# Second attention block: input projections with 512 moving weight columns, and the work between attention units dealt out anew

## The chip, the cores and the metric

One core of a Trainium2 chip runs the whole program in one launch. The metric is the device time of one execution in microseconds (us). Kernels are compared by the median of several runs.

## What is computed

The program is a chain of two transformer blocks on 512 tokens of width D = 1024, in fp32. The first block (attention with a convolution branch, then an expert layer) isn't touched here and takes the first 1866 us. The second block is this, cut to what matters:

```
h = rms_norm(x, norm_g)                       # 512 x 1024
proj = h @ w_in                               # mq mk mv mg (512 each), dq dk dv dg (512 each)
mq, mk = rms_norm per head of 64              # 8 heads
m_out = moba_attention(mq, mk, mv, slopes) * silu(mg)
dq, dk = rms_norm per component of 64         # 4 heads x 2 components
d_out = diff_attention(dq, dk, dv, lam)       # (softmax(q1 k1) - lam softmax(q2 k2)) v, causal, ALiBi
d_out = rms_norm(d_out, diff_subln) * 0.8 * silu(dg)
x = x + concat(m_out, d_out) @ w_out
```

## The kernel before, in words

Every product in fp32 is made of three TensorE matmuls on parts in the type fp32r: high x high, high x low and low x high. A weight block is loaded by DMA (`wraw`), ACT makes its high part (`whi`, L76) and DVE its low part (`wlo`, L77), both in `split`. The normed input of the second block lies transposed, feature chunk by feature chunk, in `h3h` and `h3l` (eight chunks k of 128 features by 512 tokens); they are made at the start of the block from `h3t` (L914), ACT for the high part, DVE for the low part.

The block's projections are generators, whose `yield`s are the steps in which they are dealt out. `head64` makes q or k of two head pairs (256 weight columns) for all four token tiles: `nat` (L82 to L98) takes 128 tokens as the stationary operand and 256 weight columns as the moving one, with two token tiles in each of two PSUM banks. Then come squares (ACT) with a sum (DVE), `rsq` (a square root on ACT, which loads another table, and small DVE steps), and `qn` (L973, DVE); `turn64` transposes `qn` on PE (L987) and writes qT or kT in two parts. `vals` makes v in the same way, without a norm. `gates` makes a block of 128 gate features for all 512 tokens (L113 to L115, the weights stationary and 512 token columns moving) and ends with Silu on ACT.

The attention is cut into 32 units: the kind (m, d), the head pair or diff head j (0 to 3), and the query tile qt (0 to 3). `score` makes two score tiles (three matmuls each on PE, L1027, then bias and maximum on DVE, L1032, Exp on ACT, L1036, and scaling on DVE). `turn` transposes the probabilities (L1068), and ACT copies them to `cpt`. After qt = 3, `finish` multiplies with v (`pv`, L1077 or L1081). For a diff head it has a chain of its own: `do` (ACT), `dsq` (ACT square), `ones_sum` (PE, L143), `diag` (DVE, four `ddj`, L151), `rsq` (ACT root, L125, and DVE), `bcast_rows` (PE, L137, of `drr`), then two products on DVE and the split into `mxd`. The mixed heads are multiplied with w_out: six of eight chunks in `part_out`, the last two in the last stage.

The loop over the units works two units of scores ahead (L = 2) and between them takes steps of the generators in `fill`: a number of steps `work[i]`, dealt evenly over the units up to `ends[i]`. Only q, k, v of the first pairs and gate 0 are made ahead of the loop. What stands on an engine's queue follows this order, with priorities by which a scheduler moves instructions past each other. PSUM has eight banks: three for `pm` (projections, ones, bcast, outputs), two for `s` (scores), two for `t` (turns), one for `o`.

Of the kernel before, what the change touches and what calls it, by code (L numbers as in the profile page):

```python
# [11 lines left out]
F32 = mybir.dt.float32  # L12
F32R = mybir.dt.float32r
# [17 lines left out]
def block_mixer_kernel(ctx: ExitStack, tc: tile.TileContext, a, out, dbg=None, stop=None):  # L31
# [8 lines left out]
    def pm(tag="pm"):  # L40
        return ps[0].tile([128, 512], F32, name=tag, tag=tag, bufs=ps[1][tag] if isinstance(ps[1], dict) else ps[1])
# [46 lines left out]
    def nat(src, jobs):  # L88


        for i in range(2):
            hi, lo = wsplit(src[:, 4 * i:4 * i + 4, :], 4, 256)
            for n, (o, x) in enumerate(jobs):
                for k in range(4):
                    (xh, xl), f, l = x(4 * i + k), i + k + n % 2 == 0, 4 * i + k == KD - 1
                    P.matmul(o, xh, hi[:, k, :], start=f, stop=False, skip_group_check=True)  # L96
                    P.matmul(o, xh, lo[:, k, :], start=False, stop=False, skip_group_check=True)  # L97
                    P.matmul(o, xl, hi[:, k, :], start=False, stop=l, skip_group_check=True)  # L98
                if n % 2:
# [175 lines left out]
    def tok(src, t):  # L275
        return lambda k: src(k, slice(t * 128, t * 128 + 128))
# [672 lines left out]
    p4x_tag = ["pm", "s"]

    def p4x():
        tag = p4x_tag[0]
        p4x_tag.append(p4x_tag.pop(0))
        p = [pm(tag), pm(tag)]
        return p, [(p[t // 2][:, t % 2 * 256:t % 2 * 256 + 256], tok(hx3, t)) for t in range(NT)]

    def head64(nm, b, base, gcol):

        pp, jobs = p4x()
        yield from nat(a["w_in_2n"][base + b], jobs)  # L960
        q2 = pc.tile([128, 2, 2, T], F32R, name=nm + "T", tag="T_%s%d" % (nm[1], b))
        qk[nm, b] = q2
        ss = sm.tile([128, 16], F32, name="ss64", tag="hss", bufs=2)
        for t2 in range(2):
            sq = sb.tile([128, 512], F32, name="sq64", tag="tmp", bufs=4)
            S.activation(sq, pp[t2], AF.Square)
            V.tensor_reduce(ss[:, 8 * t2:8 * t2 + 8], sq.rearrange("p (h d) -> p h d", d=64), axis=AX.X, op=OP.add)
        V.tensor_scalar(ss, ss, 1.0 / 64, EPS, op0=OP.mult, op1=OP.add)
        r = rsq(ss, 16, "r64")
        qn = []  # L970
        for t2 in range(2):
            q = sb.tile([128, 512], F32, name="qn64", tag="tmp", bufs=4)
            V.tensor_tensor(q.rearrange("p (h d) -> p h d", d=64), pp[t2].rearrange("p (h d) -> p h d", d=64),  # L973
                            r[:, 8 * t2:8 * t2 + 8, None].to_broadcast([128, 8, 64]), op=OP.mult)
            qn.append(q)
        late.append((nm, q2, qn, gcol))

    late = []

    def turn64():  # L980
        while late:
            nm, q2, qn, gcol = late.pop(0)
            for t2 in range(2):
                p2 = pm("t")
                for i in range(2):
                    for c in range(2):
                        P.transpose(p2[:, (c * 2 + i) * 128:(c * 2 + i) * 128 + 128],  # L987
                                    qn[t2][:, i * 256 + c * 128:i * 256 + c * 128 + 128], ident)
                hi = q2[:, :, 0, t2 * 256:t2 * 256 + 256]
                lo = q2[:, :, 1, t2 * 256:t2 * 256 + 256]  # L990
                p3 = p2.rearrange("p (c q) -> p c q", c=2)
                S.activation(hi, p3, AF.Copy, scale=g64[:, gcol:gcol + 1])
                V.scalar_tensor_tensor(lo, p3, g64[:, gcol:gcol + 1], hi.bitcast(F32), op0=OP.mult, op1=OP.subtract)

    def vals(nm, b, base):
        pp, jobs = p4x()
        yield from nat(a["w_in_2n"][base + b], jobs)
        v = pc.tile([128, NT, 256], F32, name=nm + "s", tag="T_v%d" % b)
        vs[nm, b] = v
        for t2 in range(2):  # L1000
            S.activation(v[:, 2 * t2:2 * t2 + 2, :], pp[t2].rearrange("p (t n) -> p t n", t=2), AF.Copy)

    def gates(j):
        w = wfeat(a["w_in_2f"][j])
# [11 lines left out]
    def both(kind, j, qt, btab):  # L1016


        w_ = (qt + 1) * 128
        wm_ = max(w_, 256)  # L1020
        q_, k_ = (qk[kind + z, j // 2][:, j % 2] for z in "qk")
        qs = slice(qt * 128, qt * 128 + 128)
        s = [pm("s"), pm("s")]
        for n, (x, y) in enumerate(((0, 0), (0, 1), (1, 0))):
            for half in range(2):
                r = slice(half * 64, half * 64 + 64)
                P.matmul(s[half][:, :wm_], q_[r, x, qs], k_[r, y, :wm_], start=n == 0, stop=n == 2)  # L1027
        r_ = []
        for half in range(2):
            st = sm.tile([128, 4], F32, name="ast", tag="ast", bufs=8)  # L1030
            e = pc.tile([128, 512], F32, name="e2", tag="e2", bufs=8)
# [77 lines left out]

    def chain(*gens):  # L1110
        for g_ in gens:
            for n, _ in enumerate(g_):
                if n == 1:
                    turn64()
                yield
        turn64()

    mxm = sb.tile([128, 2, 4, T], F32R, name="mxm", tag="xs")
    mxd = {}
    run(chain(head64("mq", 0, 0, 0), head64("mk", 0, 2, 1), vals("mv", 0, 4), gates(0)))  # L1120
# [5 lines left out]
    def part_out(j):  # L1126
# [6 lines left out]
        for k in range(6):  # L1133
# [13 lines left out]
    cur, done, total, n0, n1 = iter(()), 0, 0, 0, 1
# [78 lines left out]
def _pack(i):  # L1226
# [30 lines left out]
    p["w_in_2n"] = _blk(np.concatenate([w[:, :1536], w[:, 2048:3584]], 1), 256)  # L1257
# [22 lines left out]
```

## Time and profile before

| | |
|---|---|
| median of 3 runs | 2186.14 us (2185.35 to 2186.24) |
| the profiled execution | 2186.87 us, span 2184.9 us |
| granted clock, mean of the span | 0.991 |
| PE busy in the span | 2138.0 us (98%) |
| DVE, ACT busy in the span | 1688.1 us (77%), 1053.9 us (48%) |

The second block runs from about 1866 us to the end. Times in the rows below are microseconds from the span's start. In the timeline, "idle before" tells for how long an engine stood idle ahead of an instruction and which instruction released it. A busy PE is not PE at its peak: the ends of matmuls are modelled, so the spacing of the starts is what counts. The granted clock is a share of the full 2.4 GHz.

### The profile page before, as it was taken

Reading aid. Unit: us, or ns where it says so; the run is one execution under the profiler, and the core shown is the slowest. Engines: PE = TensorE matmul, PEld = TensorE weight load, DVE = VectorE, ACT = ScalarE, POOL = GpSimd, SP = SyncE. Lnnn points to the kernel's source line nnn. Section 1 sums busy time; section 2 is a strip of 40 time slices with the busy share of each in tenths; the row PEclk is TensorE's granted clock in tenths of the full one; section 3 lists DMA queues with packets and bytes.
Section 4 is the critical chain, followed back from the end, with each engine's and each line's share of the span. In section 5 each row is a group of like instructions: output and inputs, shape, how many; then the busy total and the mean of one; then the engine's idle time right before and its main releaser. Section 6 shows DMA issues by size and latency. Waiting matters only on the chain.

```text
span 2184.9 us, 31138 instructions
## 1 busy us (share of the span) xinstructions
PE 2138.0 (98%) x11665; PEld 1864.3 (85%) x11665; DVE 1688.1 (77%) x3340; ACT 1053.9 (48%) x1923; POOL 158.9 (7%) x132
## 2 busy tenths in 40 slices
PE   7999999999999899999999999999999999999999
PEld 3899888877688899998988889988989887888876
DVE  3999997576799999767777777787777765755564
ACT  3344367642433488734444444444443444466672
POOL 0000000000000000011111221111111100000000
PEclk9999999999999999999999999999999999999999
DMA  7322450167333266788888898898888874322221
GB/s 272 119 78 88 135 180 14 45 221 256 137 96 101 76 225 256 286 326 313 320 319 318 313 323 307 314 334 309 320 303 314 314 250 155 112 82 88 73 75 65
DMA packets 150870, 449.50 MB, mean 206 GB/s; under 512 B 12096, under 2 KB 69184, under 8 KB 131520
## 3 DMA queue, kind: packets, MB, share of 16 engines
q1 hardware_dynamic: 132288, 313.30, 41.8%
q0 software_dynamic: 18432, 134.23, 16.2%
q8 instruction: 91, 1.49, 0.3%
q14 instruction: 59, 0.48, 0.1%
HBM read 407.51 MB, written 39.98 MB: 205 GB/s over the span
## 4 chain that ended last, share of the span: by engine, by line
PE 88%; DVE 7%; ACT 2%; DMA 2%; issue 1%; SPq 0%; DVEq 0%; ACTq 0%
PE pda L770 16%; PE pm L113 9%; PE pm L115 9%; PE pm L114 9%; PE pdb L770 8%; PE pda L113 3%; PE pda L115 3%; PE pda L114 3%; PE pda L729 3%; PE pdb L113 2%; PE pdb L115 2%; PE pdb L114 2%; PE pm L430 2%; PE pm L96 2%; PE pm L97 2%; PE pm L98 2%
## 5 line engine op out<-in xcount | busy, mean ns | idle before, releaser
L76 ACT ACTIVATE whi<-wraw 128x1024 fp32r<-128x1024 f32 (+1 forms) x254 | 266.3, 1049 | 349.1 <-PE pda L114 117.5
L113 PE MATMUL pm<-h2h,whi 128*128 128x384 f32 x1024 | 347.2, 339 | 2.9 <-ACT gn L623 2.9
L77 DVE TENSOR_TENSOR wlo<-wraw,whi 128x1024 fp32r<-128x1024 f32 (+1 forms) x254 | 307.2, 1210 | 53.1 <-ACT whi L76 52.1
L115 PE MATMUL pm<-h2h,wlo 128*128 128x384 f32 x1024 | 345.1, 337 | 0.1
L114 PE MATMUL pm<-h2l,whi 128*128 128x384 f32 x1024 | 344.5, 336 | 0.0
L783 POOL DMA_INDIRECT uv<-in_peer_uv,eid x128 | 158.7, 1240 | 1606.9 <-ACT xt L724 910.4
L77 DVE TENSOR_TENSOR vvl<-vraw,vvh 128x1024 fp32r<-128x1024 f32 x128 | 156.6, 1223 | 110.7 <-ACT vvh L76 110.7
L113 PEld LDWEIGHTS pm<-h2h,whi 128*128 128x128 f32 x1024 | 193.8, 189 | 7.0 <-ACT gn L623 3.3
L114 PEld LDWEIGHTS pm<-h2l,whi 128*128 128x128 f32 x1024 | 193.7, 189 | 3.6
L115 PEld LDWEIGHTS pm<-h2h,wlo 128*128 128x128 f32 x1024 | 193.3, 189 | 0.3 <-DVE wlo L77 0.3
L814 DVE SCALAR_TENSOR_TENSOR xt<-uv,zz,xt 128x1024 f32<-128x1024 f32 x128 | 164.0, 1282 | 13.8 <-ACT zz L813 13.8
L76 ACT ACTIVATE ah<-gn 128x384 fp32r<-128x384 f32 x93 | 48.9, 526 | 232.7 <-DVE gn L756 197.5
L770 PE MATMUL pda<-vvh,ah 128*128 128x512 f32 x512 | 158.3, 390 | 0.0
L770 PE MATMUL pda<-vvl,ah 128*128 128x512 f32 x512 | 158.0, 390 | 0.0
L770 PE MATMUL pda<-vvh,al 128*128 128x512 f32 x512 | 157.6, 389 | 0.0
L786 DVE SCALAR_TENSOR_TENSOR xt<-uv,xn 128x1024 f32<-128x1024 f32 x128 | 155.9, 1218 | 0.0
L76 ACT ACTIVATE vvh<-vraw 128x1024 fp32r<-128x1024 f32 x128 | 134.5, 1051 | 5.1 <-PE pm L114 3.2
L770 PEld LDWEIGHTS pda<-vvh,ah 128*128 128x128 f32 x512 | 96.1, 188 | 21.1
L770 PEld LDWEIGHTS pda<-vvl,ah 128*128 128x128 f32 x512 | 96.1, 188 | 20.7
L770 PEld LDWEIGHTS pda<-vvh,al 128*128 128x128 f32 x512 | 96.1, 188 | 20.4
L623 ACT ACTIVATE gn<-pm 128x384 f32<-128x384 f32 x115 | 56.0, 487 | 116.4 <-PE pm L115 115.0
L77 DVE TENSOR_TENSOR al<-gn,ah 128x384 fp32r<-128x384 f32 x93 | 52.6, 565 | 66.5 <-ACT ah L76 66.5
(523 smaller groups left out, 4862.9 us busy)
## 6 DMA issues: line engine op xcount, KB each, us to landing
wraw<-in_peer_uT SPq DMA_DIRECT2D x128, 512.0 KB
vraw<-in_peer_uv SPq DMA_DIRECT2D x128, 512.0 KB
w_d<-wst SPq DMA_DIRECT2D x12, 2048.0 KB
wcur<-w_d SPq DMA_DIRECT2D x31, 768.0 KB
wraw<-in_w_in_f SPq DMA_DIRECT2D x32, 512.0 KB
mraw<-in_w_modT SPq DMA_DIRECT2D x24, 512.0 KB
wraw<-in_w_in_2n SPq DMA_DIRECT2D x24, 512.0 KB
fw<-in_w_mod SPq DMA_DIRECT2D x16, 512.0 KB
```

Source lines behind the costliest of these rows:

```text
L76: S.activation(hi, src, AF.Copy)
L77: V.tensor_tensor(lo, src, hi.bitcast(F32), op=OP.subtract)
L96: P.matmul(o, xh, hi[:, k, :], start=f, stop=False, skip_group_check=True)
L113: P.matmul(o, lh, rh, start=first, stop=False)
L114: P.matmul(o, lh, rl, start=False, stop=False)
L115: P.matmul(o, ll, rh, start=False, stop=last)
L623: S.activation(g_, p[:, :ND], AF.Gelu)
L729: P.matmul(p[:, q * 128:q * 128 + 128], o0[:, q], o1[:, q], start=True, stop=True)
L770: P.matmul(yp[t][:, d * 512:d * 512 + 512], x[:, t * 128:t * 128 + 128], v[:, d * 512:d * 512 + 512], start=j == 0 and n == 0, stop=j == N ...
L783: G.indirect_dma_start(out=uv, out_offset=None, in_=a["peer_uv"], in_offset=bass.IndirectOffsetOnAxis(ap=eid[:, s_:s_ + 1], axis=0))
L786: V.scalar_tensor_tensor(junk, uv[:, :D], 1.0, xn, op0=OP.mult, op1=OP.mult, accum_out=zs)
L814: V.scalar_tensor_tensor(y0, uv[:, D:], cs, y0, op0=OP.mult, op1=OP.add)
```

## The change

The input projections of the second block for q, k and v come in six blocks of 512 weight columns instead of twelve of 256. `nat512` walks over the token tiles outside: each token tile has a PSUM bank of its own, and the block's weights stay in four chunks, which are made while token tile 0 runs. `heads64` makes q and k together, with the norm for every two token tiles; `turn64` comes two steps later (`late`, `tick`). `vals` makes v of all four pairs. Ahead of the loop only q, k of the first pairs and gate 0 are made; v follows in the first stretch of the loop. The fill has three stretches instead of four (from units 0, 8 and 24), and gates 6 and 7 come in the last, ahead of the output steps. v of m and d have buffers of their own; `e2` has seven buffers instead of eight. The weights are packed in the new order on the host.

```diff
+    def nat512(n, done):
+        w = []
+        for t in range(NT):
+            o = pm()
+            for c in range(4):
+                if t == 0:
+                    w.append(wsplit(a["w_in_2n"][n][:, 2 * c:2 * c + 2, :], 2, 512))
+                for k in range(2):
+                    mm3(o, tok(hx3, t)(2 * c + k), [z[:, k, :] for z in w[c]], c + k == 0, c + k == 4)
+                if c == 1:
+                    yield
+            done(t, o)
+            yield
...
-        for t2 in range(2):
-            S.activation(v[:, 2 * t2:2 * t2 + 2, :], pp[t2].rearrange("p (t n) -> p t n", t=2), AF.Copy)
+        def done(t, o):
+            for b in range(2):
+                S.activation(vs[kind + "v", b][:, t, :], o[:, b * 256:b * 256 + 256], AF.Copy)
...
     def chain(*gens):
         for g_ in gens:
-            for n, _ in enumerate(g_):
-                if n == 1:
+            for _ in g_:
+                tick[0] += 1
+                if late and late[0][-1] <= tick[0] - 2:
                     turn64()
                 yield
-        turn64()
...
-    run(chain(head64("mq", 0, 0, 0), head64("mk", 0, 2, 1), vals("mv", 0, 4), gates(0)))
+    run(chain(heads64("m", 0, 0), gates(0)))
...
-    fill = {0: chain(head64("mq", 1, 0, 0), head64("mk", 1, 2, 1), gates(1), vals("mv", 1, 4), gates(2), gates(3)),
-            8: chain(head64("dq", 0, 6, 2), head64("dk", 0, 8, 3), vals("dv", 0, 10), gates(4), gates(5)),
-            16: chain(head64("dq", 1, 6, 2), head64("dk", 1, 8, 3), vals("dv", 1, 10), gates(6), gates(7)),
-            25: chain(*(part_out(j) for j in range(KD)))}
-    ends = {0: 8, 8: 16, 16: 25, 25: 38}
-    work = {0: 18, 8: 16, 16: 16, 25: 8}
+    fill = {0: chain(vals("m", 1), heads64("m", 1, 2), gates(1)),
+            8: chain(gates(2), heads64("d", 0, 3), gates(3), vals("d", 4), gates(4), heads64("d", 1, 5), gates(5)),
+            24: chain(gates(6), gates(7), *(part_out(j) for j in range(KD)))}
+    ends = {0: 8, 8: 24, 24: 36}
+    work = {0: 18, 8: 32, 24: 12}
...
+        while late and i + L in (8, 16, 24):
+            turn64()
         if i + L < len(units):
             e[i + L] = score(units[i + L])
```

Three pieces of the engines' order follow: the line, the operation, the tiles and the shape. The line numbers are those of the kernel that the piece comes from; after the change L96 to L98 become L113 to L115, and the others move by 14 to 16.

PE at the finish of diff head 0, before: `o` is `pv`, `ones` the sum, `drr` the broadcast; `pm<-whi,h3h` and its like are projections.

```order
L1077 MATMUL o<-cpt,dvs 128x128
L1068 MATMUL t<-ident,e_18138 128x128
L987 MATMUL t<-ident,qn_18252 128x128 x4
L96 MATMUL pm<-whi,h3h 128x256
...
L987 MATMUL t<-ident,qn_18254 128x128 x4
L143 MATMUL pm<-dsq,ones 128x512
L97 MATMUL pm<-wlo,h3h 128x256
...
L1027 MATMUL s<-dkT,dqT 128x512 x6
L1068 MATMUL t<-ident,e_18218 128x128 x2
L1068 MATMUL t<-ident,e_18297 128x128 x3
L1027 MATMUL s<-dkT,dqT 128x256 x10
L137 MATMUL pm<-ident,drr 128x128 x4
```

The same place after the change:

```order
L1093 MATMUL o<-cpt,dvs 128x128
L1084 MATMUL t<-ident,e_17546 128x128
L1043 MATMUL s<-dkT,dqT 128x512 x6
L1001 MATMUL t<-ident,qn_17681 128x128 x4
L1001 MATMUL t<-ident,qn_17683 128x128 x4
L143 MATMUL pm<-dsq,ones 128x512
L1043 MATMUL s<-dkT,dqT 128x256 x2
L1084 MATMUL t<-ident,e_17623 128x128 x2
L1043 MATMUL s<-dkT,dqT 128x256 x10
L137 MATMUL pm<-ident,drr 128x128 x4
L113 MATMUL pm<-whi,h3h 128x512
```

Before, 10 projection matmuls stood ahead of the sum and 14 between the sum and the broadcast; after, they all stand behind the broadcast.

ACT at the same finish, before: `do` and `dsq` of the chain, `drt` the root, `e` the Exp of scores (its number tells the tile), `r64t` the root for q and k.

```order
L125 ACTIVATE r64t<-ss_18237 128x16
L1036 ACT_TABLE_LOAD
L1036 ACTIVATE e_18297,ast<-e_18297,ast 128x384
L1036 ACTIVATE e_18300,ast<-e_18300,ast 128x384
L1092 ACTIVATE do<-o 128x512
L1069 ACTIVATE cpt<-t 128x128
L1094 ACTIVATE dsq<-do 128x512
L992 ACTIVATE dkT<-t,g_15885 128x2x256 x2
L1001 ACTIVATE dvs<-pm 128x512
L125 ACT_TABLE_LOAD
L125 ACTIVATE drt<-ddv 128x4
```

And after the change:

```order
L1052 ACTIVATE e_17697,ast<-e_17697,ast 128x384
L1085 ACTIVATE cpt<-t 128x128
L1052 ACTIVATE e_17792,ast<-e_17792,ast 128x512
L1108 ACTIVATE do<-o 128x512
L1052 ACTIVATE e_17795,ast<-e_17795,ast 128x512
L1110 ACTIVATE dsq<-do 128x512
L1006 ACTIVATE dqT<-t,g_15885 128x2x256
L1006 ACTIVATE dkT<-t,g_15885 128x2x256
L1085 ACTIVATE cpt<-t 128x2x128
L1052 ACTIVATE e_17877,ast<-e_17877,ast 128x128
L1052 ACTIVATE e_17880,ast<-e_17880,ast 128x128
L125 ACT_TABLE_LOAD
```

Two Exps of 512 columns now stand ahead of `dsq`, and two of 128 with a copy ahead of the root's table; the copy `dvs` and one `dkT` are gone from between.

PE at the finish of diff head 1, after the change; `pm<-h3h,whi` and its like are gate 6.

```order
L1093 MATMUL o<-cpt,dvs 128x128
L1084 MATMUL t<-ident,e_17877 128x128
L115 MATMUL pm<-h3h,wlo 128x512
L113 MATMUL pm<-h3h,whi 128x512
...
L143 MATMUL pm<-dsq,ones 128x512
L1043 MATMUL s<-dkT,dqT 128x512 x6
L1084 MATMUL t<-ident,e_17936 128x128 x2
L1084 MATMUL t<-ident,e_17982 128x128 x3
L1043 MATMUL s<-dkT,dqT 128x256 x12
L1043 MATMUL s<-dkT,dqT 128x384 x6
L1043 MATMUL s<-dkT,dqT 128x512 x3
L137 MATMUL pm<-ident,drr 128x128 x4
```

Ten matmuls of gate 6 stand between `pv` and the sum, where before there were only scores and turns; the other 14 of gate 6 stand ahead of `pv`, and gate 7 behind the broadcast.

## Rows read from the trace of the kernel before

**Rows 1.** Windows: us; busy of PE, PEld, DVE, ACT, POOL (instructions); PEclk; DMA share; GB/s.

```profile
1867.00:1877.00 10.00, 9.89 (x60) 9.60 (x61) 9.88 (x19) 5.55 (x10) 0.00 (x0) 0.71 0.01 2
1912.00:2075.00 163.00, 161.85 (x1205) 142.11 (x1204) 92.72 (x258) 107.79 (x202) 0.00 (x0) 1.00 0.26 81
2075.00:2092.00 17.00, 16.82 (x117) 13.56 (x117) 13.93 (x53) 14.37 (x27) 0.00 (x0) 1.00 0.24 82
2105.00:2130.00 25.00, 22.51 (x96) 14.96 (x95) 17.43 (x76) 19.84 (x44) 0.00 (x0) 0.86 0.11 32
2121.95:2128.78 6.83, 6.82 (x19) 4.90 (x19) 5.46 (x23) 4.42 (x13) 0.00 (x0) 0.50 0.01 2
```

**Rows 2.** Groups by line of PE, 1866 to 2185 us: shapes, count | busy, mean ns | idle.

```profile
L96 PE MATMUL pm<-whi,h3h 128*128 128x256 f32 x352 | 102.5, 291 | 1.1 <-DVE qn L973 0.9
...
L98 PE MATMUL pm<-whi,h3l 128*128 128x256 f32 x352 | 99.9, 284 | 0.0
...
L96 PE MATMUL s<-whi,h3h 128*128 128x256 f32 x32 | 10.0, 312 | 0.1
```

**Rows 3.** Timeline of PE, 256 columns: start us, us; first and last of 60 matmuls.

```profile
1878.06 0.29 PE L96 MATMUL pm<-whi,h3h 128*128 128x256 f32 x1
...
1885.14 0.28 PE L98 MATMUL pm<-whi,h3l 128*128 128x256 f32 x1
```

**Rows 4.** Timeline of PE, 512 columns: first and last of 21 matmuls.

```profile
2031.78 0.39 PE L113 MATMUL pm<-h3h,whi 128*128 128x512 f32 x1
...
2036.31 0.39 PE L115 MATMUL pm<-h3h,wlo 128*128 128x512 f32 x1
```

**Rows 5.** Timeline of DVE at the block's start: the last chunk's low part.

```profile
1876.09 0.69 DVE L77 TENSOR_TENSOR h3l<-h3t,h3h 128x512 fp32r<-128x512 f32 x1
```

**Rows 6.** Waits of PE and its weight loads, 1866 to 2185 us: total, times, longest.

```profile
PE pm L96 <- DVE qn L973: 0.9, 3, 0.4
...
PEld pm L96 <- DVE qn L973: 1.4, 2, 0.7
```

**Rows 7.** Timeline of PE at the finish of diff head 0.

```profile
2079.87 2.42 PE L1077 MATMUL o<-cpt,dvs 128*128 128x512 f32 x8
...
2084.43 1.02 PE L143 MATMUL pm<-dsq,ones 128*128 128x512 f32 x2
...
2090.72 0.65 PE L137 MATMUL pm<-ident,drr 128*128 128x128 f32 x4
```

**Rows 8.** Groups by line and shape of ACT, 1866 to 2185 us.

```profile
L1036 ACT ACT_TABLE_LOAD x16 | 20.5, 1283 | 1.5 <-DVE ast L1032 0.7 <-DVE r64t L127 0.5
...
L1036 ACT ACTIVATION_READ_ACCUMULATOR e<-e,ast 128x1 f32 x64 | 12.1, 189 | 0.0
...
L1036 ACT ACTIVATE e<-e,ast 128x512 f32<-128x512 f32 x16 | 11.4, 720 | 0.2 <-DVE ast L1032 0.2
...
L1036 ACT ACTIVATE e<-e,ast 128x384 f32<-128x384 f32 x16 | 9.7, 607 | 0.9 <-DVE ast L1032 0.9
...
L1036 ACT ACTIVATE e<-e,ast 128x128 f32<-128x128 f32 x16 | 6.3, 395 | 0.3 <-DVE ast L1032 0.2
...
L1094 ACT ACTIVATE dsq<-do 128x512 f32<-128x512 f32 x4 | 2.5, 631 | 0.0
```

**Rows 9.** Timeline of PE at the finish of diff head 1.

```profile
2109.72 2.42 PE L1077 MATMUL o<-cpt,dvs 128*128 128x512 f32 x8
...
2124.09 1.12 PE L137 MATMUL pm<-ident,drr 128*128 128x128 f32 x4
```

**Rows 10.** Timeline of PE at the finishes of diff heads 2 and 3.

```profile
2139.03 2.32 PE L1077 MATMUL o<-cpt,dvs 128*128 128x512 f32 x8
...
2146.59 0.65 PE L137 MATMUL pm<-ident,drr 128*128 128x128 f32 x4 [0.47 <-DVE drr L129]
...
2155.26 1.02 PE L143 MATMUL pm<-dsq,ones 128*128 128x512 f32 x2
...
2160.05 0.65 PE L137 MATMUL pm<-ident,drr 128*128 128x128 f32 x4 [0.71 <-DVE drr L129]
```

More of the change, by code (lines that the diff above doesn't have):

```diff
@@ L948, in block_mixer_kernel @@
     LAST_TAGS = "s", "s", "t", "t", "o", "pm", "pm", "pm"
[L949 to L963, printed above, removed]
-        for t2 in range(2):
[L965 to L976, printed above, removed]
@@ L978, in block_mixer_kernel @@
-    late = []
-    def turn64():
[L981 to L1000, printed above, removed]
-            S.activation(v[:, 2 * t2:2 * t2 + 2, :], pp[t2].rearrange("p (t n) -> p t n", t=2), AF.Copy)
+    def nat512(n, done):
[11 more added lines that the diff above has]
+            yield
@@ new lines, in heads64 @@
+    def heads64(kind, b, n):
+        for z in "qk":
+            qk[kind + z, b] = pc.tile([128, 2, 2, T], F32R, name=kind + z + "T", tag="T_%s%d" % (z, b))
+        pp = []
+        def done(t, o):
+            pp.append(o)
+            if t % 2 == 0:
+                return
+            ss = sm.tile([128, 16], F32, name="ss64", tag="hss", bufs=2)
+            for i in range(2):
+                sq = sb.tile([128, 512], F32, name="sq64", tag="tmp", bufs=4)
+                S.activation(sq, pp[i], AF.Square)
+                V.tensor_reduce(ss[:, 8 * i:8 * i + 8], sq.rearrange("p (h d) -> p h d", d=64), axis=AX.X, op=OP.add)
+            V.tensor_scalar(ss, ss, 1.0 / 64, EPS, op0=OP.mult, op1=OP.add)
+            r = rsq(ss, 16, "r64")
+            qn = []
+            for i in range(2):
+                q = sb.tile([128, 512], F32, name="qn64", tag="tmp", bufs=4)
+                V.tensor_tensor(q.rearrange("p (h d) -> p h d", d=64), pp[i].rearrange("p (h d) -> p h d", d=64),
+                                r[:, 8 * i:8 * i + 8, None].to_broadcast([128, 8, 64]), op=OP.mult)
+                qn.append(q)
+            pp.clear()
+            late.append((kind, b, t // 2, qn, tick[0]))
+        yield from nat512(n, done)
@@ new lines, in block_mixer_kernel @@
+    late, tick = [], [0]
+    def turn64():
+        kind, b, t2, qn, _ = late.pop(0)
+        for n, z in enumerate("qk"):
+            q2, gcol = qk[kind + z, b], n + 2 * (kind == "d")
+            p2 = pm("t")
+            for i in range(2):
+                for c in range(2):
+                    P.transpose(p2[:, (c * 2 + i) * 128:(c * 2 + i) * 128 + 128],
+                                qn[i][:, n * 256 + c * 128:n * 256 + c * 128 + 128], ident)
+            hi = q2[:, :, 0, t2 * 256:t2 * 256 + 256]
+            lo = q2[:, :, 1, t2 * 256:t2 * 256 + 256]
+            p3 = p2.rearrange("p (c q) -> p c q", c=2)
+            S.activation(hi, p3, AF.Copy, scale=g64[:, gcol:gcol + 1])
+            V.scalar_tensor_tensor(lo, p3, g64[:, gcol:gcol + 1], hi.bitcast(F32), op0=OP.mult, op1=OP.subtract)
@@ L1003, in gates, with vals, done @@
+    def vals(kind, n):
+        for b in range(2):
+            vs[kind + "v", b] = pc.tile([128, NT, 256], F32, name=kind + "vs", tag="T_%sv%d" % (kind, b))
+        def done(t, o):
+            for b in range(2):
+                S.activation(vs[kind + "v", b][:, t, :], o[:, b * 256:b * 256 + 256], AF.Copy)
+        yield from nat512(n, done)
     def gates(j):
@@ L1030, in both @@
             st = sm.tile([128, 4], F32, name="ast", tag="ast", bufs=8)
-            e = pc.tile([128, 512], F32, name="e2", tag="e2", bufs=8)
+            e = pc.tile([128, 512], F32, name="e2", tag="e2", bufs=7)
             V.tensor_tensor_reduce(out=e[:, :w_], in0=s[half][:, :w_], in1=btab[half][:, 512 - w_:], scale=-0.125, scalar=BIG,
@@ L1136, in part_out @@
         yield
-    fill = {0: chain(head64("mq", 1, 0, 0), head64("mk", 1, 2, 1), gates(1), vals("mv", 1, 4), gates(2), gates(3)),
-            8: chain(head64("dq", 0, 6, 2), head64("dk", 0, 8, 3), vals("dv", 0, 10), gates(4), gates(5)),
-            16: chain(head64("dq", 1, 6, 2), head64("dk", 1, 8, 3), vals("dv", 1, 10), gates(6), gates(7)),
-            25: chain(*(part_out(j) for j in range(KD)))}
-    ends = {0: 8, 8: 16, 16: 25, 25: 38}
-    work = {0: 18, 8: 16, 16: 16, 25: 8}
-    p4x_tag[:] = ["pm"]
+    fill = {0: chain(vals("m", 1), heads64("m", 1, 2), gates(1)),
[3 more added lines that the diff above has]
+    work = {0: 18, 8: 32, 24: 12}
     L = 2
@@ L1184, in block_mixer_kernel @@
             if k == 1:
-                o = pc.tile([128, 512], F32, name="o", tag="e2", bufs=8)
+                o = pc.tile([128, 512], F32, name="o", tag="e2", bufs=7)
                 V.tensor_tensor(o, last_p[j], part[j // 4][:, j % 4, :], op=OP.add)
@@ L1256, in _pack @@
     w = i["w_in_2"][0]
-    p["w_in_2n"] = _blk(np.concatenate([w[:, :1536], w[:, 2048:3584]], 1), 256)
+    at = [(0, 512), (1024, 1280), (256, 768), (2048, 2560), (3072, 3328), (2304, 2816)]
+    p["w_in_2n"] = _blk(np.concatenate([w[:, c:c + 256] for x in at for c in x], 1), 512)
     p["w_in_2f"] = _blk(np.concatenate([w[:, 1536:2048], w[:, 3584:]], 1), 128)
```

## Prediction

> **What bounds the kernel now.** I read the windows of the second block first [rows 1]: each row gives a stretch, then the busy time of PE, PEld, DVE, ACT and POOL, and PE's granted clock. In the long middle, 1912 to 2075 us, PE is busy 161.85 of 163 us at full clock, so there time is the number of matmuls times their spacing, and ACT (107.79) and DVE (92.72) have room. At two places it is not so. Near 2105 to 2130 ACT is busy 19.84 of 25 us, PE 22.51, and the clock is 0.86: at 2121.95 to 2128.78 it is 0.50, the level 1.2 GHz. And at the block's start, 1867 to 1877, the clock is 0.71 and DVE has 9.88 of 10 us busy: there PE is paced by DVE, which makes `h3h`/`h3l`. The kernel is thus a PE sum plus holes at the start and at the four finishes of the diff heads. The change works on both, so I price both.
>
> **Part 1, wider weight columns.** The line groups [rows 2] list 352 matmuls of L96 into `pm` and 32 into `s`, and L97 and L98 have as many: 1152 of 256 columns. After the change there are 576 of 512. Their spacing on PE: from 1878.06 to 1885.14 us there are 59 steps of 256 columns, 0.120 us each [rows 3]; from 2031.78 to 2036.31 us 20 steps of 512 columns, 0.2265 us each [rows 4]. A column costs 0.417 ns at the full clock (2.4 GHz), so both rows leave the same 13 ns per matmul over their columns, and halving the count saves that 576 times. The sum: 1152 x 0.120 = 138.2 us, 576 x 0.2265 = 130.5 us; **-7.7 us**. The first of those matmuls at low clock make it a little less; I take **-7.5**. [...]
>
> The Trainium skill, page "TensorE: Matmul & The Clock Gate", section "Back-to-back issue gap", gives an isolated gap of N/2.4 + 2.5 ns, which speaks against this part: by it 1152 x 109.2 ns against 576 x 215.8 ns, an estimate of 1.5 us gained. The trace disagrees with its 120 and 226.5 ns.
>
> Twice as many `vals` copies of half the size (16 of 256 columns for 8 of 512), and as many squares, reductions and `qn` as before: these lie on ACT and DVE in the middle, where both have room; at nothing. If that cover were gone, the 8 more copies at 0.4 us would be 3 us. The weights' bytes and DMAs are the same; 8 buffers of `e2` to 7 matter only where scores run far ahead, which L = 2 does not; nothing.
>
> **Part 2, the start.** Before, two blocks share each chunk k of `h3`, so eight token-tile products follow each chunk. After, token tile 0 alone walks through all eight chunks, and the last chunk's `h3l` is made from 1876.09 [rows 5]; the matmuls of tiles 1 to 3 wait behind it in the order. In the window 1867 to 1877 the row counts 60 matmuls [rows 1], 7.2 us' worth at 0.120, and a few records can be missing. After, tile 0's 24 and a few of tile 1 behind them, about 29 by the order, can be done: 29 x 0.2265 = 6.6 us. I take **+1.0**, a little over the difference of 0.6 for the missing records; ends +0.5 and +4 (the tile stalls, and the low clock lasts 3 us longer).
>
> **Part 3, the waits for `qn`.** PE waited 0.9 us in all for `qn` [rows 6], and its weight loads another 1.4. Now a pair of token tiles has its norm while the next pair's matmuls (5.4 us instead of 2.9) run, so these go: **-1.8**, between -0.9 and -2.3.
>
> **Part 4, the finish of diff head 0.** Chain: `pv` on PE, `do` and `dsq` on ACT, `ones` on PE, `ddj` on DVE, root on ACT (with a table load each way), `bcast` on PE. Before, `pv` began at 2079.87, ended 2.42 later at 2082.29, and `bcast` came at 2090.72: 8.4 us, of which PE filled about 6.7 with 24 weight-column matmuls (24 x 0.120 = 2.9), scores, turns and `ones` [rows 7]; 1.7 lost. After, the order leaves no projection there: between `pv` and `bcast` stand 12 score matmuls of 512 and 256 (0.9 + 1.1), eight `qn` turns (1.2), `ones` (1.0) and three `e` turns (0.3): 4.5 us.
>
> And the gap itself grows, for ACT's order has more in it. I walk it from the end of token tile 1 (t = 0), with the durations of [rows 8]: square to 0.7; two `e` of 384 around a root table, root and exp table (1.28 each) end at 5.9, since the root needs both reductions (0.69); `cpt` 6.2; one `e` of 512 (0.72 + 0.19) 7.1; `do` 7.7; the second `e` 8.6; `dsq` 9.2. `ones` ends at 10.2, four `ddj` at 12. Meanwhile `dqT` and `dkT` (0.68 each), and only then the scores of the next block's first unit, their two `e` (0.6 each with the read), which stand ahead of the root on ACT: to about 14.1. Table 1.28, root 0.2, small DVE steps 0.7 and `bcast` at 17.1. `pv` ended at 3.0: the gap is **14.1 us**, work 4.5, loss 9.6 instead of 1.7: **+7.9**. Bounds: the gap stays 8.4, loss 3.9, +2.2; with the 12.0 us that head 1 now takes [rows 9], 7.5, +5.8. I take the walk since its order on ACT is fixed.
>
> **Part 5, heads 1 to 3.** Head 1: from the end of `pv` (2109.72 + 2.4) to `bcast` 2124.09 [rows 9] is 12.0 us, in which PE had scores only. After, ten matmuls of gate 6 stand there: 10 x 0.2265 = **-2.3**; the other 38 of the two gates stand ahead or behind. Head 2: `pv` of head 3 stood in the gap (2.4 us) and leaves it: `pv` ended at 2141.4 and `bcast` at 2146.59 [rows 10], 5.2 us with 1.4 lost; the order after has turns, 3 scores and `ones`, some 3.6 us, in a gap that an exp table and two `e` lengthen to about 7.2: loss 3.6, **+2.2**; ends 0 and +6. Head 3: before, 12 matmuls of the last stage stood between `ones` 2155.26 and `bcast` 2160.05 [rows 10]; after, they stand behind. The gap of 5.2 holds 1.0 of work, 4.2 lost against 1.2: **+3.1**.
>
> **Part 6, the clock.** After head 1's thin stretch the clock went to 0.50 for 6.8 us with some 3.9 us' worth of full-rate matmuls in it [rows 1]. Head 0's hole is now as thin: one more such stretch, of which half falls on waiting anyway: **+1.8**; half a chance of another at heads 2 and 3: **+0.9**. Ends 0 and +6.
>
> **The sum:** -7.5 + 1.0 - 1.8 + 7.9 - 2.3 + 2.2 + 3.1 + 1.8 + 0.9 = +5.3. The profiled execution took 2186.87 us (its span 2184.9 and 2.0 around it), 0.7 above the median of the runs, 2186.14; so 2192.2 on its scale, **2191.4** on the median's.
>
> **The rivals.**
> - *The gaps keep their old length: faster.* If `dsq` reaches PE within 2.3 us of `pv`'s end, as in the trace before, heads 0 and 2 cost +2.2 and +1 and no clock falls: -7.5 + 1.0 - 1.8 + 2.2 - 2.3 + 1.0 + 2.5 = -4.9, 2181. For it: before, ACT served that chain in 8.4 us. Against it: the two more `e` of 512 ahead of `dsq` and two of 128 ahead of the root. It decides at whether ACT is behind when `pv` ends.
> - *About as before.* Head 0's gap is 12.0 (+5.8), and no further stretch at low clock comes: +5.3 - 2.1 - 2.7 = +0.5, with head 2 at half price -0.6: 2185 to 2188.
> - *The columns gain little.* Part 1 is worth 1.5 to 2.3 and the rest is as forecast: +10.5 to +11.3, near 2197. Rows 3 and 4 speak against it. The isolated gap of the page above is this rival's rule.
> - *The kept gates don't do what they are kept for.* If all 48 matmuls of gates 6 and 7 stood in head 1's hole, its loss would go: 10 us of holes less about 5 more than I count, 2186. The order shows ten there.
>
> **How the numbers follow.** About 0.2%, 4.4 us, is what a measurement of this kernel can tell from no change. My forecast, with its neighbours above +4.4, 0.33; the columns gaining little or yet more low clock, 0.15; about as before (with the kept gates doing more) 0.30; the gaps keeping their length 0.22. So faster 0.22, same 0.30, slower 0.48. The range leaves out 1 in 10 on each side: from 2179.5 (the faster rival with the upper `qn` bound) to 2198 (low clock at 0 to 3, or small column gain). The likeliest case's own range, 2188 to 2196, comes from the bounds of head 0 and of the clock.
>
> **What would show it.** In the profile after: 576 more matmuls of 512 columns at 0.2265 us and none of 256 in `pm`; no PE wait on `qn`; from the end of head 0's `pv` to its `bcast` 14 us (8.4 says the faster rival, 12 the middle one), with PE idle there in front of `ones` and `bcast`; a granted clock of 0.5 after it; ten matmuls on a gate in head 1's gap; the last stage's matmuls behind head 3's `bcast`. Wrong would be: `ones` of head 0 within 3 us of `pv`'s end, a spacing above 0.235 us, or a stall of PE at 1870 to 1880 of more than 4 us.

## The result and the profile after

The kernel after the change takes 2199.91 us (median of 4 runs, 2197.77 to 2201.18), beside 2185.74 us of the kernel before (4 runs): a ratio of 1.0064, 95% interval 1.0052 to 1.0076. Slower was forecast, by 5.3 us; it is 14.2 us, and 2199.91 lies above the range (2179.5 to 2198.0).

The page's head and the first parts of the profile after:

```profile
span 2198.8 us, 29981 instructions
PE 2139.0 (97%) x11089; PEld 1834.8 (83%) x11089; DVE 1692.4 (77%) x3340; ACT 1054.6 (48%) x1930; POOL 161.1 (7%) x132
```

The profiled execution took 2200.83 us with a span of 2198.8 us, 13.9 more than before. The broadcast that opens the second block started at 1864.45 us before and at 1865.07 after, so the first block accounts for 0.6 of that and the second block for 13.3 (PE's timelines, before and after):

```profile
1864.45 1.12 PE L137 MATMUL pm<-ident,n4r 128*128 128x128 f32 x4 [3.99 <-DVE n4r L908]
...
1865.07 0.65 PE L137 MATMUL pm<-ident,n4r 128*128 128x128 f32 x4 [3.99 <-DVE n4r L908]
```

The windows, as in [rows 1] (us; busy of PE, PEld, DVE, ACT, POOL; PE's granted clock; DMA):

```profile
1867.00:1877.00 10.00, 8.30 (x27) 6.39 (x28) 9.88 (x19) 5.71 (x10) 0.00 (x0) 0.71 0.01 2
1912.00:2066.00 154.00, 153.12 (x803) 116.08 (x804) 88.34 (x239) 98.08 (x196) 0.00 (x0) 1.00 0.26 83
2066.40:2083.60 17.20, 11.03 (x46) 6.62 (x45) 12.73 (x54) 12.94 (x28) 0.00 (x0) 0.73 0.32 123
2075.00:2088.00 13.00, 10.33 (x31) 6.70 (x31) 9.11 (x38) 6.40 (x15) 0.00 (x0) 0.51 0.12 49
2134.00:2146.00 12.00, 8.36 (x34) 5.84 (x33) 7.51 (x24) 7.13 (x12) 0.00 (x0) 0.86 0.22 67
2157.00:2170.00 13.00, 9.02 (x29) 6.18 (x28) 5.76 (x18) 2.91 (x5) 0.00 (x0) 0.74 0.09 31
```

The middle is as full as before, 153.12 of 154 us. The holes are at the finishes of heads 0, 2 and 3 (11.03 of 17.2 us, 8.36 of 12, 9.02 of 13), each with a lowered clock, and in the first row PE did 27 matmuls in 10 us.

First and last of 27 matmuls of a wide projection, on PE's timeline:

```profile
1888.36 0.39 PE L113 MATMUL pm<-whi,h3h 128*128 128x512 f32 x1
...
1894.28 0.39 PE L115 MATMUL pm<-whi,h3l 128*128 128x512 f32 x1
```

26 steps in 5.92 us are 0.2277 us each, where 0.2265 was forecast [rows 4]. That term came nearly as said: at 0.2277, 576 of them save 7.1 us against 1152 at 0.120.

PE at the finish of head 0, which answers to [rows 7]:

```profile
2066.41 2.42 PE L1093 MATMUL o<-cpt,dvs 128*128 128x512 f32 x8
...
2068.87 0.97 PE L1043 MATMUL s<-dkT,dqT 64*128 64x512 f32 x6
2072.62 1.16 PE L1001 MATMUL t<-ident,qn 128*128 128x128 f32 x8 [2.78 <-DVE qn L984]
2074.51 2.07 PE L143 MATMUL pm<-dsq,ones 128*128 128x512 f32 x2 [0.72 <-ACT dsq L1110]
...
2082.53 1.12 PE L137 MATMUL pm<-ident,drr 128*128 128x128 f32 x4 [2.18 <-DVE drr L129]
2083.30 0.78 PE L113 MATMUL pm<-whi,h3h 128*128 128x512 f32 x1
```

From the end of `pv` (2068.8) to the broadcast are 13.7 us without one projection matmul, and PE waits: 2.78 us for `qn`, 0.72 for `dsq`, 2.18 for `drr`. The clock had fallen inside the gap: `ones` takes 2.07 us, where it took 1.02 before [rows 7]. The first projection stands right behind the broadcast. ACT's timeline of the same stretch shows the walk of the prediction nearly to the tenth:

```profile
2072.65 0.58 ACT L1108 ACTIVATE do<-o 128x512 f32<-128x512 f32 x1
...
2073.84 0.62 ACT L1110 ACTIVATE dsq<-do 128x512 f32<-128x512 f32 x1
...
2079.84 1.28 ACT L125 ACT_TABLE_LOAD   x1
2081.13 0.20 ACT L125 ACTIVATE drt<-ddv 128x4 f32<-128x4 f32 x1
```

The last matmul of token tile 1 started at 2065.38, so the tile had ended at 2065.6; from there `do` ends at 7.6 (7.7 was forecast), `dsq` at 8.9 (9.2), the root comes at 15.5 (15.4), the broadcast at 16.9 (17.1).

PE at the finishes of heads 2 and 3, beside [rows 10]:

```profile
2138.29 1.02 PE L143 MATMUL pm<-dsq,ones 128*128 128x512 f32 x2
2142.95 1.09 PE L1084 MATMUL t<-ident,e 128*128 128x128 f32 x4 [3.64 <-DVE drr L126]
2143.84 1.06 PE L137 MATMUL pm<-ident,drr 128*128 128x128 f32 x4
...
2157.52 2.32 PE L1093 MATMUL o<-cpt,dvs 128*128 128x512 f32 x8
2161.19 1.13 PE L143 MATMUL pm<-dsq,ones 128*128 128x512 f32 x2 [1.35 <-ACT dsq L1110]
2164.95 1.12 PE L137 MATMUL pm<-ident,drr 128*128 128x128 f32 x4 [2.63 <-DVE drr L129]
```

At head 2, four turns of the last unit stand ahead of the broadcast on PE's queue and wait 3.64 us. The row puts this down to `drr`, which the turns don't read; what they read was scaled on DVE just before, to 2142.81:

```profile
2142.06 0.75 DVE L1075 SCALAR_TENSOR_TENSOR e<-e,ast,e 128x512 f32<-128x512 f32 x1
```

At head 3 nothing stands between, and PE waits 1.35 and 2.63 us.

To compare kernels I split the second block's PE time into work (each matmul by the spacing of its shape at full clock, 0.120 and 0.2265 us for projections of 256 and 512 columns, [rows 3] and [rows 4]) and what is lost beside it (waits and low clock). Worked out from the timelines, in us; the start is the first 48 us, the middle goes to head 0's `pv`, the finishes to the end:

```
                                        work   start  middle  finishes  block
before                                 289.8     4.6     8.2      14.1  316.7
after                                  282.1     7.6     7.4      33.0  330.0
e1_width  (wide, old dealing)          282.1     6.8     7.7      25.3  321.8
e2_deal   (256, new dealing)           289.8     5.4     5.3      20.4  320.9
e3_split                               282.1     7.8     7.6      23.0  320.5
e4_start                               282.1     4.8     7.4      32.2  326.5
e9_before_obank  (256, old)            289.8     4.5     8.2       5.1  307.6
e13_deal_obank   (256, new)            289.8     5.4     5.3       8.9  309.4
e10_width_obank  (wide, old)           282.1     6.8     7.7       7.2  303.8
e7_obank         (wide, new)           282.1     8.1     7.6       6.5  304.3
e8_obank_start   (wide, new)           282.1     5.4     7.6       6.6  301.6
e12_best         (wide, old)           282.1     3.9     7.8       7.2  300.9
e11_first                              282.1     8.1     7.4      19.5  317.1
e14_touch                              283.7     7.7     7.7      12.0  311.1
```

So the change saves 7.8 of work (the difference of the unrounded sums) and 0.8 in the middle, and gives back 3.0 at the start and 18.9 at the finishes. Each row is one profiled execution. That of `e1_width` took 2192.84 us, 6.7 more than the median of its runs, so its 25.3 is more than a usual run lost; that of `e8_obank_start` took 5.9 more than its median. Which matmuls stand in a gap is read from the same trace and comes from the program's order.

### The profile page after: what moved, and what is told of

Read it like the earlier page. It is cut to its first block, busy times and chain, and to the rows that moved or that the text cites. A ratio compares the mean times of both kernels' runs of the same rounds, so it can differ in the third digit from the quotient of the medians.

```text
span 2198.8 us, 29981 instructions
## 1 busy us (share of the span) xinstructions
PE 2139.0 (97%) x11089; PEld 1834.8 (83%) x11089; DVE 1692.4 (77%) x3340; ACT 1054.6 (48%) x1930; POOL 161.1 (7%) x132
## 4 chain that ended last, share of the span: by engine, by line
PE 63%; DVE 7%; ACT 2%; issue 1%; DMA 0%; DVEq 0%; ACTq 0%
PE pda L770 16%; PE pm L113 10%; PE pm L114 10%; PE pm L115 10%; PE pdb L770 8%; PE pda L729 3%; PE pdb L729 1%; DVE wlo L77 1%; PE s L1043 1%; PE t L1084 1%; PE pda L115 1%; PE pda L113 1%; PE pda L114 0%; DVE xt L680 0%; DVE xt L684 0%
## 5 line engine op out<-in xcount | busy, mean ns | idle before, releaser
L113 PE MATMUL pm<-h2h,whi 128*128 128x384 f32 x1024 | 346.4, 338 | 2.7 <-ACT gn L623 2.7
L115 PE MATMUL pm<-h2h,wlo 128*128 128x384 f32 x1024 | 344.6, 337 | 0.9 <-DVE wlo L77 0.9
L113 PEld LDWEIGHTS pm<-h2h,whi 128*128 128x128 f32 x1024 | 193.1, 189 | 6.8 <-ACT gn L623 3.2
L115 PEld LDWEIGHTS pm<-h2h,wlo 128*128 128x128 f32 x1024 | 192.9, 188 | 1.6 <-DVE wlo L77 1.6
L814 DVE SCALAR_TENSOR_TENSOR xt<-uv,zz,xt 128x1024 f32<-128x1024 f32 x128 | 164.2, 1282 | 13.7 <-ACT zz L813 13.7
```

Of the source, the lines that this page charges most:

```text
L113: P.matmul(o, lh, rh, start=first, stop=False)
L115: P.matmul(o, ll, rh, start=False, stop=last)
L814: V.scalar_tensor_tensor(y0, uv[:, D:], cs, y0, op0=OP.mult, op1=OP.add)
```

## The experiments

**Width and dealing apart.** Two theories stood against each other: the dealt order empties the finishes, or the wide blocks cost wherever they are dealt.

```diff
 # e1_width: the kernel after, dealt out as before
-    run(chain(heads64("m", 0, 0), gates(0)))
+    run(chain(heads64("m", 0, 0), vals("m", 1), gates(0)))
+    fill = {0: chain(heads64("m", 1, 2), gates(1), gates(2), gates(3)),
+            8: chain(heads64("d", 0, 3), vals("d", 4), gates(4)),
+            16: chain(heads64("d", 1, 5), gates(5), gates(6), gates(7)),
+            25: chain(*(part_out(j) for j in range(KD)))}
+    ends = {0: 8, 8: 16, 16: 25, 25: 38}
+    work = {0: 14, 8: 18, 16: 14, 25: 8}
```

> The wide projections alone: 512 columns as in the change, but the steps dealt out as before (v of m ahead of the loop, four stretches, gates 6 and 7 in the third). Order theory (the loss comes from what stands, or no longer stands, in the finishes and at the start): the columns give 7.7 us, the start still costs 2.9, so near 2181 us (2177 to 2184). Width theory (blocks of 512 cost wherever they are dealt: one bank per token tile, larger pieces): 2190 us or more.

Measured: 2186.14 us (2183.36 to 2193.24), ratio to before 0.9999 (0.999 to 1.0009). That is neither theory's number.

```diff
 # e2_deal: the kernel before, dealt out as after (v with tags of its own, e2 bufs 7)
+    fill = {0: chain(vals("mv", 0, 4), vals("mv", 1, 4), head64("mq", 1, 0, 0), head64("mk", 1, 2, 1), gates(1)),
+            8: chain(gates(2), head64("dq", 0, 6, 2), head64("dk", 0, 8, 3), gates(3), vals("dv", 0, 10),
+                     vals("dv", 1, 10), gates(4), head64("dq", 1, 6, 2), head64("dk", 1, 8, 3), gates(5)),
+            24: chain(gates(6), gates(7), *(part_out(j) for j in range(KD)))}
+    ends = {0: 7, 8: 23, 24: 36}
...
```

> The dealing alone: projections of 256 columns as before, in the change's order (v of m in the loop, three stretches, gates 6 and 7 last). Order theory: the kernel after, plus 7.7 us for the columns, less the 2.9 of the start, so near 2204 us (2199 to 2208). Width theory: within 2 us of the kernel before, 2184 to 2188 us.

Measured: 2190.52 us (2188.05 to 2197.22), ratio 1.002 (1.0009 to 1.0031), again neither theory's number. Alone, the width is worth nothing and the dealing costs about 4 us, yet both together cost 14. What tells more is head 0's hole in each. PE's timeline of `e1_width`, wide with the old dealing:

```profile
2077.72 2.42 PE L1093 MATMUL o<-cpt,dvs 128*128 128x512 f32 x8
2086.85 1.94 PE L143 MATMUL pm<-dsq,ones 128*128 128x512 f32 x2
...
2094.56 3.93 PE L1093 MATMUL o<-cpt,dvs 128*128 128x512 f32 x8
2099.19 0.65 PE L137 MATMUL pm<-ident,drr 128*128 128x128 f32 x4
```

and PE's groups by line between the end of `pv` and the broadcast of `e2_deal`, 256 columns with the new dealing (count | busy, mean ns | idle):

```profile
L96 PE MATMUL pm<-whi,h3h 128*128 128x256 f32 x24 | 7.3, 302 | 0.0
L98 PE MATMUL pm<-whi,h3l 128*128 128x256 f32 x24 | 6.9, 286 | 0.0
L97 PE MATMUL pm<-wlo,h3h 128*128 128x256 f32 x24 | 6.8, 282 | 0.0
```

In `e1_width` the broadcast comes 21.5 us after `pv` started, behind `pv` of the next head, with no projection in between. In `e2_deal` 72 stand in the gap and PE hardly waits. So head 0's hole comes with the width and not with the dealing. At heads 2 and 3 it is the other way round: `e2_deal`, with 256 columns, waits there nearly as the kernel after does (PE's timeline):

```profile
2131.63 0.63 PE L1068 MATMUL t<-ident,e 128*128 128x128 f32 x4 [2.77 <-DVE e L1059]
...
2150.73 1.13 PE L143 MATMUL pm<-dsq,ones 128*128 128x512 f32 x2 [1.35 <-ACT dsq L1094]
2154.50 0.90 PE L137 MATMUL pm<-ident,drr 128*128 128x128 f32 x3 [2.64 <-DVE drr L129]
```

No weight-column matmul stands between `pv` and the broadcast of these two heads there, as in the kernel after. What may set `e1_width` and `e2_deal` apart at head 0 is when a PSUM bank is taken: 256 columns take both banks of a block together, at its first matmuls, so the rest of the block is free to run; a wide block takes a bank per token tile, as a gate or an output block takes one each. New theory: banks of one tag are handed out in the program's order, and the broadcast takes its own only when it can run; a token tile that comes behind it in the program gets no bank until then.

**Filling the hole by program order, and the start.**

```diff
 # e3_split: the finish from the broadcast on is issued one unit later, behind that unit's fill
-        rb = bcast_rows(rsq(v, NT, "dr"), NT)
+        r = rsq(v, NT, "dr")
+        rest.append(lambda: ending(h, t, r))
...
```

> The kernel after, with the second half of a diff head's finish (from the broadcast on) issued one unit later, behind that unit's fill; in the order 24 projection matmuls (24 x 0.2265 = 5.4 us) then stand between ones and the broadcast of head 0. Order theory: 5 us of head 0's waits and its 2.3 us of low clock go, heads 1 and 2 gain 1 to 3 more: near 2191 us (2187 to 2194). If the chain of head 0 is not what PE waits for (the scores of the next unit are): 2198 to 2201 us.

Measured: 2191.86 us (2188.8 to 2193.81), ratio 1.0023 (1.0013 to 1.0032): as the order theory said. The bank theory would have said the same, as the broadcast now takes its bank behind that unit's fill; the run doesn't tell the two apart.

```diff
 # e4_start: first block, chunks outside, four token tiles inside, banks s, s, t, o
+            o4 = [pm(x) for x in tags]
+            for c in range(4):
+                z = wsplit(a["w_in_2n"][n][:, 2 * c:2 * c + 2, :], 2, 512)
+                for t in range(NT):
+                    for k in range(2):
+                        mm3(o4[t], tok(hx3, t)(2 * c + k), [y[:, k, :] for y in z], c + k == 0, c + k == 4)
...
```

> The kernel after, with the block ahead of the loop walking over the chunks outside and the four token tiles inside, in four PSUM banks (s, s, t, o), so that PE waits neither for a free bank nor for the last chunk. Order theory: the start's extra 2.9 us go: 2197 us (2195.5 to 2198). If the start is paced by the making of h3 alone: no change, 2199 to 2201 us.

Measured: 2197.52 us (2195.07 to 2198.56), ratio 1.0048 (1.0031 to 1.0064): the start's loss falls from 7.6 to 4.8 us, to that of before (4.6). The edit changes the walk and the banks together, so this run doesn't tell which of them it is. In the kernel after, PE stands twice at the start for a bank (PE's timeline):

```profile
1868.70 0.79 PE L113 MATMUL pm<-whi,h3h 128*128 128x512 f32 x1 [1.99 <-ACT lam L940]
...
1882.60 0.47 PE L113 MATMUL pm<-whi,h3h 128*128 128x512 f32 x1 [0.54 <-DVE xs L921]
```

The first wide matmul waits 1.99 us until ACT has read `lam` out of its bank, and a later token tile until DVE has read the last `xs` product. The prediction had priced the start by the order and by `h3` alone.

**The bank theory, tested from three sides.** First the finish leaves the `pm` ring (the three banks of that tag, which are handed out in turn):

```diff
 # e7_obank: ones and the broadcast of a diff head in the bank of pv
...
-        p = ones_sum(lambda k: sq, 1, T)
+        p = ones_sum(lambda k: sq, 1, T, pm("o"))
-        rb = bcast_rows(rsq(v, NT, "dr"), NT)
+        rb = bcast_rows(rsq(v, NT, "dr"), NT, pm("o"))
```

> The kernel after, with the ones sum and the broadcast of a diff head's finish in the bank of pv (tag o) instead of two of the three pm banks; nothing else. Bank theory (with one pm bank per token tile, handed out in the program's order, the next token tile gets its bank only once the broadcast has its own, so the projections can't stand ahead of it): in the order 32, 20, 21 and 28 weight-column matmuls now stand between pv and the broadcast of heads 0 to 3, 0, 10, 0 and 0 in the kernel after; head 0's 10 us and most of the holes of heads 1 to 3 go, with the low clock behind them: near 2178 us (2174 to 2183). Dealing theory (the dealt order leaves the finish's own chain on the path): 2190 us or more.

Measured: 2173.76 us (2172.67 to 2174.98), ratio 0.9944 (0.9927 to 0.9961), 26 us under the kernel after and just under the bank theory's range. PE's timeline at head 0, and its groups between `pv` and the broadcast:

```profile
2066.86 2.42 PE L1093 MATMUL o<-cpt,dvs 128*128 128x512 f32 x8
2073.76 1.02 PE L143 MATMUL o<-dsq,ones 128*128 128x512 f32 x2
...
2080.49 0.62 PE L137 MATMUL o<-ident,drr 128*128 128x128 f32 x4 [0.28 <-DVE drr L129]
```

```profile
L113 PE MATMUL pm<-whi,h3h 128*128 128x512 f32 x11 | 4.6, 415 | 0.0
L114 PE MATMUL pm<-wlo,h3h 128*128 128x512 f32 x11 | 4.4, 400 | 0.0
L115 PE MATMUL pm<-whi,h3l 128*128 128x512 f32 x10 | 4.3, 434 | 0.0
```

The gap is 11.2 us long, but 32 projection matmuls stand in it, and only 0.28 us of waiting is left at its end. ACT's and DVE's work are the same as in the kernel after. The finishes lose 6.5 us instead of 33.0.

The same edit in the kernel before (`e9_before_obank`):

> The kernel before with the ones sum and the broadcast in the bank of pv, nothing else. Bank theory: the 8.6 us of head 1 and 1 to 3 us of heads 2 and 3 go: near 2177 us (2174 to 2181), about as far as the change with the same edit and 512 columns. Dealing theory: 2184 to 2187 us.

Measured: 2177.72 us (2175.95 to 2181.43), ratio 0.9963 (0.9952 to 0.9975), as the bank theory said. Its finishes fall from 14.1 to 5.1, most of it at head 1, where no projection had been in the gap either.

The same edit in `e1_width` (`e10_width_obank`):

> The wide projections dealt out as before, with the ones sum and the broadcast in the bank of pv. Bank theory: what the 512 columns save is then seen whole: the kernel before with the same edit less 7.7 us, plus 2 to 3 at the start, near 2172 us (2169 to 2178). Width theory (blocks of 512 cost elsewhere too): within 2 us of the kernel before with the same edit, or slower.

Measured: 2171.68 us (2170.72 to 2173.61), ratio 0.9939 (0.9922 to 0.9955), as the bank theory said.

And the same in `e2_deal` (`e13_deal_obank`):

> Projections of 256 columns, dealt out as in the change, with the ones sum and the broadcast in the bank of pv: the fourth corner beside the three runs with that edit. With the holes filled the dealing should be worth nothing: as the kernel before with that edit, 2177.7 us (2175 to 2181), and the 512 columns 4 to 6 us under it in either dealing (7.7 saved, 2 to 3 given back at the start).

Measured: 2179.89 us (2177.38 to 2182.86), ratio 0.9972 (0.9963 to 0.9982). In this set of four the width takes 6 us off in either dealing (2177.7 to 2171.7, 2179.9 to 2173.8), and the dealing adds 2 in either width, about what the runs can tell. By the length of the block in the table the width takes 3.8 and 5.1 off. With the holes filled, the two parts add up; without, they didn't.

But a free bank is also one bank more. So two edits that leave the finish in the `pm` ring and change little but when a bank is taken (the first also moves three matmuls a token tile forward, the second adds one matmul a head):

```diff
 # e11_first: the next token tile's first product goes ahead of done(t, o), and isn't made again in its own tile
...
+            if t + 1 < NT:
+                nxt = pm()
+                mm3(nxt, tok(hx3, t + 1)(0), [z[:, 0, :] for z in w[0]], True, False)
             done(t, o)
```

> The kernel after, with the first product (three matmuls) of each next token tile issued ahead of the step's end, so that the next tile has taken its bank before a finish takes its own; nothing else, and the finish keeps its pm banks. In the order 21, 11, 0 and 0 weight-column matmuls then stand between pv and the broadcast of heads 0 to 3 (0, 10, 0, 0 in the kernel after). Bank theory: head 0's hole shrinks by 21 x 0.2265 = 4.8 us and its 2.2 us of low clock go: near 2193 us (2189 to 2195). If it was the freed pm banks that counted in the runs with tag o, and not the turn in which they are handed out: 2198 us or more.

Measured: 2187.57 us (2184.43 to 2192.87), ratio 1.0008 (0.9999 to 1.0018): 12 us under the kernel after, more than said. Head 0's loss (waits and the clock after) falls from 12.5 to 2.4 us: nine projections now stand ahead of the `qn` turns, which come 4.4 us after `pv` started instead of 6.2, and no wait for `qn` is left. Head 2's loss stays, as its order said.

```diff
 # e14_touch: one useless matmul takes the broadcast's bank early
+        pb = pm()
+        P.matmul(pb[:, :128], ones, ident, start=True, stop=True)
-        rb = bcast_rows(rsq(v, NT, "dr"), NT)
+        rb = bcast_rows(rsq(v, NT, "dr"), NT, pb)
```

> The kernel after, with one useless matmul of 128 columns into the broadcast's bank, issued right behind the ones sum, so that the bank is taken early; nothing is left out and one matmul a head is added. In the order 24, 20, 18 and 11 weight-column matmuls then stand between pv and the broadcast. Bank theory: 5.4 us at head 0, 2.3 at head 1, 4.1 at head 2 and 2.5 at head 3, and some 4 us of low clock: near 2182 us (2178 to 2187). If the number of banks counted: 2199 to 2201 us.

Measured: 2182.13 us (2180.39 to 2185.31), ratio 0.9983 (0.9973 to 0.9992): a matmul more, and 18 us less than the kernel after. PE at head 0 there, with the useless matmul at 2076.66:

```profile
2074.79 2.07 PE L143 MATMUL pm<-dsq,ones 128*128 128x512 f32 x2 [0.26 <-ACT dsq L1110]
2076.66 0.48 PE L1115 MATMUL pm<-ident,ones 128*128 128x128 f32 x2
...
2082.43 0.60 PE L137 MATMUL pm<-ident,drr 128*128 128x128 f32 x4
```

The broadcast comes 13.3 us after `pv`'s end, as in the kernel after, and 24 projections stand ahead of it. The number of banks is unchanged, so it's the turn in which they are taken that empties the gaps of projections. It isn't quite all of what `e7_obank` gained: the finishes lose 12.0 us here and 6.5 there. Whether the rest comes from the bank more or from the smaller number of projections in the gaps (24, 20, 18 and 11 against 32, 20, 21 and 28) wasn't told apart.

**A version that beats both.** `e7_obank` with `e4_start`'s first block (`e8_obank_start`):

> As the run before, and with the first block over four banks with the chunks outside. Bank theory: the 2 to 3 us that this gave in the kernel after come on top: near 2175 us (2171 to 2180). Dealing theory: 2187 us or more.

Measured: 2169.77 us (2169.35 to 2175.66), ratio 0.9927 (0.991 to 0.9943), 16 us under the kernel before and under the range.

The old dealing, `e10_width_obank`, with `e4_start`'s first block (`e12_best`):

> The wide projections dealt out as before, with the ones sum and the broadcast in the bank of pv and the first block over four banks with the chunks outside: 2171.7 us less the 2 to 4 us that the start gave elsewhere, near 2169 us (2166 to 2171), the same within noise as the change with these two edits (2169.8).

Measured: 2173.34 us (2171.34 to 2174.79), ratio 0.9939 (0.9923 to 0.9956). That misses its range, and is above the 2171.68 of `e10_width_obank`, on which it was to gain. By the table its block does take less, 300.9 us against 303.8; in the two profiled executions it began at 1868.40 and 1861.67 us, so the difference lies ahead of the block. That of `e8_obank_start` takes 301.6; the medians, from two chips, don't tell the two versions apart.

## Why the prediction fell short

The sign and the place were right, and so was most of what one would see: no projection in head 0's gap, a gap of 13.7 us (14.1 forecast), a clock of 0.5 behind it, ten gate matmuls at head 1, the last stage behind head 3's broadcast. Against it, PE did wait for `qn`, 3.5 us in all where it had waited 0.9 before. The number was outside the range because most terms for what is lost were sized too small, nearly all on one side:

- **Projections**, -7.5: -7.1 by the 0.2277 us of the trace after, and -7.8 in the table, which counts 0.2265 and puts the rest to the losses. The rival by which the columns gain little falls with that; no run shows its 2.3 us. The isolated gap in the Trainium skill, page "TensorE: Matmul & The Clock Gate", section "Back-to-back issue gap", from which the prediction estimated 1.5 us, doesn't fit either: by it 512 columns would take an estimated 215.8 ns, and the trace after shows 227.7.
- **The start**, +1.0: measured +3.0, inside its end of +4. The step took PE to be paced by `h3`; two waits for a PSUM bank, 1.99 and 0.54 us, weren't in it. `e4_start` takes 2.8 of it back. The row of before has PE busy 9.89 of 10 us at a clock of 0.71 [rows 1], so there PE was slowed by its clock more than by waiting for `h3`.
- **The `qn` waits**, -1.8: the middle gained 0.8, and a wait of 2.78 us for `qn` came up in head 0's hole.
- **Head 0 and its low clock**, +7.9 and +1.8: measured +11.9. Of this +8.6 lies in the finish itself, +2.1 in the twelve matmuls behind the broadcast, which ran partly at 1.2 GHz, and +1.2 between there and the next `pv`. The gap came as walked, but the work in it is less than the 4.5 us said. It was summed from durations, whose ends are modelled and overlap; by the spacing of the starts (0.109 us a turn, 0.24 and 0.12 a pair of scores of 512 and 256 columns, 0.43 a matmul of `ones`) it is about 3.4. The order has 18 score matmuls there, six of 512 and twelve of 256, not 12.
- **Head 1**, -2.3: measured -2.9.
- **Heads 2 and 3**, +2.2, +3.1 and +0.9 for the clock: measured +9.8. Head 2 lost 5.2 us instead of 3.6: its gap of 6.9 us is no longer than the 7.2 forecast, but by their spacing the matmuls in it are worth about 2.3 us and not 3.6. Behind heads 2 and 3 the clock cost 2.7 us, not 0.9: after each of the two holes it was low, where half a chance of one had been counted.

So the step that failed is the sum over the finishes of heads 2 and 3 with the clock (6.2 forecast, 9.8 measured), then head 0's surroundings (9.7, 11.9) and the start (1.0, 3.0). The range failed with them: its upper end came from one rival at a time, though the holes' bounds all lean the same way, and a hole brings its low clock with it.

And why the holes are there was left open. The prediction read from the order that no projection stands in head 0's gap, and asked no further; the first two expectations laid it to the dealing. `e1_width` has the hole with the old dealing, `e2_deal` hasn't with the new; `e11_first` and `e14_touch` show that the turn in which `pm` banks are taken does it. The dealing by itself costs about 4 us: by the table its finishes lose 6.3 more, with the holes of heads 2 and 3 larger and that of head 1 smaller, and the middle loses 2.9 less. The gaps of heads 2 and 3 too fill when the broadcast's bank is taken early (18 and 11 matmuls in `e14_touch`, none in the kernel after).

## What to carry to other kernels

Where independent work is to cover a chain, look at what the two share besides engines: a ring of PSUM banks that is handed out in the program's order puts filler that takes its bank later in the program behind the chain's last step. Give the chain a bank of its own (here the one that its first step has just freed), or let the filler take its bank ahead of the chain; here it cost a few lines and took 8 us off the kernel before (`e9_before_obank`), more than the wide matmuls gave in any pair of runs. When an order shows a hole, count the clock behind it too, for each hole apart.

## What was not expected of the hardware

The clock went to 0.5 (1.2 GHz) in or behind short stretches in which PE had little to do. Two windows of the kernel after, columns as above, at head 3:

```profile
2160.00:2165.00 5.00, 1.18 (x3) 0.35 (x3) 2.03 (x13) 1.31 (x3) 0.00 (x0) 0.79 0.00 0
2165.70:2169.70 4.00, 4.00 (x11) 3.14 (x10) 2.13 (x3) 0.63 (x1) 0.00 (x0) 0.50 0.00 0
```

In the first, PE is busy 1.18 of 5 us, and the clock falls before its end; in the second, PE is full at half the clock, 11 matmuls in 4 us. That is 2 us for a hole of 5. Also, where the second block starts (the row of L137) lies between 1861.67 and 1868.40 us in these profiles though nothing ahead of it is changed. So medians of few runs can't tell 2 us, and the block's own length tells more.
